# Feed-forward of a decoder layer: the up projection by Strassen's seven products on three equal token chunks, the down projection as a pass of its own

## The chip, the cores and the metric

The kernel runs on one core of a Trainium2 chip. The metric is device time in microseconds (us), from the first to the last instruction of one launch; less is better.

## The reference

One inference step of a decoder layer, for a prompt of 2048 tokens and for 8 sample tokens with a paged cache. Ahead of the feed-forward there are the input projection, three mixers (sparse attention with an indexer, pooling, attention to a memory) and the output projection with its residual. The change is in the last part:

```python
D_MODEL = 1024; D_FF = 2816; CONV_WIDTH = 3
def conv_ffn(up_ext, cw, cb, wd):
    T = up_ext.shape[1] - (CONV_WIDTH - 1)
    c = cb
    for j in range(CONV_WIDTH):
        c = c + cw[j] * up_ext[:, j:j + T]
    g, val = c[..., :D_FF], c[..., D_FF:]
    return (jax.nn.silu(g) * val) @ wd
...
up = rmsnorm(xp, norm2_g[l]) @ w_up[l]        # 2048 x 1024 by 1024 x 5632
up_ext = jnp.pad(up, ((0, 0), (CONV_WIDTH - 1, 0), (0, 0)))
xp = xp + conv_ffn(up_ext, conv_w[l], conv_b[l], w_down[l])
```

The sample tokens go through the same feed-forward, each with two past rows of its own for the convolution. Everything is float32.

## The kernel before

Each float32 operand of a product is split into a high and a low part, and a product is three matmuls: high by high, high by low, low by high. The splitting is a helper: ScalarE copies the high part (L224), VectorE subtracts it from the raw value (L225). The kernel is written in a framework that schedules: each engine works through a queue whose order is fixed when the program is built, by priorities that follow the order of the code; code under a raised number (`cur_priority += 1500`) gives way to as many instructions that come later.

After the output projection the second norm's result `h` (1024 channels, 8 groups of 128) is the right operand of the up projection. The feed-forward (L1600 and on) goes over three chunks of tokens, with bounds 0, 768, 1546 and 2048, the last with the 8 sample tokens. The first chunk's high and low parts (`fhh`, `fhl`) and its residual rows (`yacc`) stay on chip from the output projection on; those of later chunks are loaded from `h_d` and `x1_d` in memory. In a chunk the loop goes over 22 blocks `f` of 128 hidden units, and in a block:

- for the gate and the value (`j`): 512 KB of weights `wr` are loaded and split into `uh` and `ul` (128x1024), and the up projection (L1675 to L1677) adds 8 channel groups x 3 matmuls in PSUM (`upg`, `upv`), in two column pieces of 384 to 390, or one of 512 in the last chunk;
- the convolution takes its bias and last tap on ScalarE (L1679), the other taps on VectorE (L1680, L1682), each reading PSUM; then Silu on ScalarE (L1691), gate by value on GpSimd (L1692, `ct`), the high part `ah` on ScalarE and the low part `al` on VectorE;
- 512 KB of down weights `dr` are split into `dh` and `dl`. Every two blocks the down projection (L1717 to L1719, 512 columns) sums the two in PSUM (`py`), and VectorE adds that to `yacc` (L1720, 408 times). The rows of `yacc` are written out after the last block.

The sample tokens' mixers are traced ahead of this with 1500 instructions of lower priority, so they run beside the first two chunks: the indexer's scores over the cache (products `ipr` on GpSimd, L1244, summed by VectorE to `dots`, L1246), a search for the 256 best (L1285 and on), gathers, attention (`sw`, L1488 and L1506), the output projection (`swo`), the norm and the write of `h_d` for the third chunk (L1574).

## Time and profile before

| what | value |
|---|---|
| time, median of 3 runs | 2964.07 us (2961.45 to 2965.29) |
| the profiled execution, span | 2975.3 us, of mean granted clock 0.970 |
| TensorE, VectorE, GpSimd, ScalarE busy | 94%, 75%, 40%, 46% of the span |
| the feed-forward | 1373.8 us to the end |
| DMA over the whole span | 301.68 MB, 101 GB/s on average |

A busy time counts the instructions that the hardware profiler recorded; matmuls overlap one another, so their durations add up to more than the time they take, and the distance of successive starts is the price of one. "PE" is TensorE, "DVE" VectorE, "POOL" GpSimd, "ACT" ScalarE, "SP" the engine whose queue issues most transfers. The granted clock is a share of TensorE's full clock of 2.4 GHz, of which 1.2 GHz is the other level. An arrow in a row names what ended the idle time ahead of the instructions.

### The profile page before, as it was taken

To read this page: it belongs to the slowest core of one execution; us is meant where nothing else is said; L and a number is where in the kernel's file an instruction comes from. 1 tells how busy PE (TensorE), PEld (TensorE's weight loads), DVE (VectorE), ACT (ScalarE), POOL (GpSimd) and SP (SyncE) were. 2 spreads that over 40 slices of the span, in tenths; PEclk is the share of its full clock that TensorE was granted. 3 is DMA by queue.
4 is the path that set the end of the run, shared out by engine and by line. 5 is a ranking of instruction groups with operands and counts; after the bars stand their busy time and mean duration, and the time that the engine had idled before them with its cause. 6 is when DMAs were issued, how large, how long until landed. Compare 5 with 4: busy or idle time off the path is not lost.

```text
span 2975.3 us, 41646 instructions
## 1 busy us (share of the span) xinstructions
PE 2787.9 (94%) x14707; PEld 2428.2 (82%) x14707; DVE 2241.5 (75%) x4459; ACT 1365.5 (46%) x2307; POOL 1187.9 (40%) x1097
## 2 busy tenths in 40 slices
PE   8988788869999999999999999999989999999997
PEld 7877456658988988888988888989878889878886
DVE  5788987967888888446899989898787665666554
ACT  5667686457777777345222222232223333233332
POOL 2333434835745564002888998310436100000000
PEclk9999899879999999999999999999999999999999
DMA  5321334372213223653222222233343322243331
GB/s 183 124 91 54 124 101 123 102 215 80 82 55 99 62 83 99 190 149 115 71 74 75 86 64 73 69 122 121 96 129 92 109 80 82 82 153 106 93 92 53
DMA packets 310311, 301.68 MB, mean 101 GB/s; under 512 B 27444, under 2 KB 272245, under 8 KB 309317
## 3 DMA queue, kind: packets, MB, share of 16 engines
q1 hardware_dynamic: 305236, 285.28, 31.2%
q0 software_dynamic: 4864, 13.73, 1.6%
q8 instruction: 116, 1.90, 0.3%
q14 instruction: 95, 0.77, 0.1%
HBM read 236.36 MB, written 62.89 MB: 101 GB/s over the span
## 4 chain that ended last, share of the span: by engine, by line
PE 58%; DVE 12%; POOL 6%; DMA 3%; issue 2%; ACT 1%; SPq 0%; DVEq 0%; ACTq 0%; POOLq 0%
POOL ipr L1244 4%; PE py L1717 4%; PE upv L1677 4%; PE upv L1675 4%; PE py L1719 4%; PE upv L1676 4%; PE py L1718 4%; PE upg L1677 4%; PE upg L1675 4%; PE upg L1676 4%; PE apt L1055 3%; PE as L1038 2%; DVE dots L1246 2%; PE ax L1058 2%; PE ax L1059 2%
## 5 line engine op out<-in xcount | busy, mean ns | idle before, releaser
L1244 POOL TENSOR_TENSOR ipr<-G,qbc 128x512 f32<-128x512 f32 x256 | 371.1, 1479 | 66.4 <-DVE dots L1246 55.4
L1032 POOL TENSOR_TENSOR t<-R,first 128x128 f32<-128x128 f32 (+15 forms) x128 | 289.0, 2290 | 209.4 <-PE apt L1055 178.9
L1692 POOL TENSOR_TENSOR ct<-ct,ct 128x768 f32<-128x768 f32 (+2 forms) x65 | 118.6, 1824 | 623.8 <-DVE ct L1686 305.6
L1720 DVE TENSOR_TENSOR yacc<-yacc,py 128x512 f32<-128x512 f32 (+1 forms) x408 | 273.1, 680 | 117.8 <-PE py L1719 95.6
L1717 PE MATMUL py<-dh,ah 128*128 128x512 f32 (+1 forms) x704 | 279.8, 399 | 16.0 <-DVE yacc L1720 10.7
L1719 PE MATMUL py<-dh,al 128*128 128x512 f32 (+1 forms) x704 | 275.3, 397 | 3.9 <-DVE al L1697 3.9
L1718 PE MATMUL py<-dl,ah 128*128 128x512 f32 (+1 forms) x704 | 278.1, 395 | 0.0
L224 ACT ACTIVATE uh<-wr 128x1024 fp32r<-128x1024 f32 x132 | 139.6, 1058 | 292.9 <-PE upv L1676 97.3
L1676 PE MATMUL upg<-fhl,uh 128*128 128x390 f32 (+3 forms) x748 | 258.0, 345 | 5.0 <-issue 3.0
L225 DVE TENSOR_TENSOR ul<-wr,uh 128x1024 fp32r<-128x1024 f32 x132 | 176.7, 1339 | 110.4 <-ACT uh L224 110.2
L1676 PE MATMUL upv<-fhl,uh 128*128 128x390 f32 (+3 forms) x748 | 256.9, 343 | 0.0
L1675 PE MATMUL upg<-fhh,uh 128*128 128x390 f32 (+2 forms) x704 | 241.0, 342 | 5.2 <-DVE ct L1682 3.5
L1675 PE MATMUL upv<-fhh,uh 128*128 128x390 f32 (+2 forms) x704 | 240.1, 341 | 3.5 <-ACT ct L1679 2.0
L1677 PE MATMUL upg<-fhh,ul 128*128 128x390 f32 (+2 forms) x704 | 240.7, 342 | 2.8 <-issue 2.8
L1677 PE MATMUL upv<-fhh,ul 128*128 128x390 f32 (+2 forms) x704 | 239.4, 340 | 0.0
L225 DVE TENSOR_TENSOR pl<-apt,ph 128x512 fp32r<-128x512 f32 (+1 forms) x320 | 204.2, 658 | 24.2 <-ACT ph L224 21.9
L1040 DVE CUSTOM_DVE_ANT_0 t<-as,t 128x512 f32<-128x512 f32 (+11 forms) x320 | 189.8, 606 | 41.9 <-PE as L1039 36.7
L224 ACT ACTIVATE ph<-apt 128x512 fp32r<-128x512 f32 (+1 forms) x320 | 173.1, 581 | 62.0 <-PE apt L1055 32.5
L1246 DVE TENSOR_REDUCE dots<-ipr 128x16 f32<-128x512 f32 x256 | 171.8, 679 | 27.5 <-POOL ipr L1244 27.2
L1717 PEld LDWEIGHTS py<-dh,ah 128*128 128x128 f32 (+1 forms) x704 | 132.7, 189 | 44.5 <-DVE yacc L1720 16.5
L1055 PE MATMUL apt<-ident,t 128*128 128x128 f32 x1088 | 164.9, 274 | 3.4 <-DVE pl L225 1.9
L353 ACT ACTIVATE rl<-isc 128x768 f32<-128x768 f32 (+9 forms) x176 | 138.0, 822 | 59.7 <-PE isc L350 42.9
(578 smaller groups left out, 7676.1 us busy)
## 6 DMA issues: line engine op xcount, KB each, us to landing
wr<-in_w_up_dram SPq DMA_DIRECT2D x132, 512.0 KB
dr<-in_w_down_dram SPq DMA_DIRECT2D x66, 512.0 KB
xt<-in_x_prompt_dram SPq DMA_DIRECT2D x16, 512.0 KB
xh_d<-xh SPq DMA_DIRECT2D x16, 512.0 KB
xl_d<-xl SPq DMA_DIRECT2D x16, 512.0 KB
xh<-xh_d SPq DMA_DIRECT2D x16, 512.0 KB
xl<-xl_d SPq DMA_DIRECT2D x16, 512.0 KB
qa<-qh_d SPq DMA_DIRECT2D x64, 128.0 KB
```

The source lines that it names most:

```text
L224: nc.scalar.activation(hi, ps, AF.Copy)
L225: nc.vector.tensor_tensor(lo, ps, hi.bitcast(F32), op=OP.subtract)
L1032: nc.gpsimd.tensor_tensor(t[:, :N], backward(R[j][:, :N]), nsel[b], op=OP.add)
L1055: nc.tensor.transpose(pt[:, c, j * 128:j * 128 + 128], pn[j][:, (k + c) * 128:(k + c) * 128 + 128], ident)
L1244: nc.gpsimd.tensor_tensor(pr, G[:, u * 512:u * 512 + 512].rearrange("p (k d) -> p k d", d=32), qbc[:, c, None, 32 * h:32 * h + 32].to_broa ...
L1675: nc.tensor.matmul(d, uh[:, k], hh(k, a, e), start=(k == 0), stop=False)
L1676: nc.tensor.matmul(d, uh[:, k], hl(k, a, e), start=False, stop=False)
L1677: nc.tensor.matmul(d, ul[:, k], hh(k, a, e), start=False, stop=(k == KC - 1))
L1717: nc.tensor.matmul(py[:p], ah[:, r0:r0 + p], dh[:, cs], start=(i == 0), stop=False)
L1718: nc.tensor.matmul(py[:p], ah[:, r0:r0 + p], dl[:, cs], start=False, stop=False)
L1719: nc.tensor.matmul(py[:p], al[:, r0:r0 + p], dh[:, cs], start=False, stop=e)
L1720: nc.vector.tensor_tensor(y[:w, cs], y[:w, cs], py[:w], op=OP.add)
```

## The change

The tokens are cut into three equal chunks: 688, 688 and 680 (the last with the sample tokens). A chunk's right operand is a matrix of two channel halves by two token halves; the left one has two channel halves by gate and value of a block. Their product is made by Strassen's scheme in Winograd's form: seven products of half size instead of eight, each of 4 channel groups x 3 matmuls at 344 (340) columns. The seven right operands (`b11`, `t1`, `t2`, `b21`, `t3`, `b22`, `t4`) are made once a chunk (`operands`: eight subtractions on GpSimd, and 14 splits) and stay on chip. The seven left operands are made for every block: three are parts of the weights as loaded, four are sums `s` made on GpSimd. Partial products are summed in place in PSUM and put together into `u` in SBUF by four copies on ScalarE and three additions on VectorE. The convolution reads `u`. The activation is written to memory (`act_d`).

The down projection is a pass of its own for each chunk and each half of the output columns: it loads the activation and the down weights, splits them, and sums all 22 blocks in PSUM; at the end the residual is loaded, added by VectorE and written. All 16 blocks of the output projection now write `x1_d` and `h_d`. The sample tokens' mixers get 5500 in place of 1500. Comments are removed throughout.

```diff
-    bounds = [0, 768, 1546, 2048]
+    chunks = [(0, 344), (688, 344), (1376, 340)]
...
+    def operands(ci, stage):
+        for kk in range(0, 4, 2):
+            get(raw("b11"), 0, 0)
+            get(x, 0, 1)
+            get(raw("b22"), 1, 1)
+            get(raw("b21"), 1, 0)
+            G(y, x, raw("b11"), op=OP.subtract)
+            split_psum(raw("b11"), h("b11"), l("b11"))
+            split_psum(y, h("t1"), l("t1"))
+            G(x, raw("b22"), x, op=OP.subtract)
+            G(y, raw("b22"), y, op=OP.subtract)
+            split_psum(y, h("t2"), l("t2"))
+            G(y, raw("b21"), y, op=OP.subtract)
+            split_psum(raw("b21"), h("b21"), l("b21"))
+            split_psum(x, h("t3"), l("t3"))
+            split_psum(raw("b22"), h("b22"), l("b22"))
+            split_psum(y, h("t4"), l("t4"))
...
-    tc.cur_priority += 1500
+    tc.cur_priority += 5500
...
+                product(pa, two_parts(g0), "b11", True)
+                nc.scalar.activation(x1, pa[:, :N], AF.Copy)
+                G(s, v0, v1, op=OP.add)
+                product(pc, two_parts(s), "t1", True)
+                nc.scalar.activation(x5, pc[:, :N], AF.Copy)
+                G(s, s, g0, op=OP.subtract)
+                product(pa, two_parts(s), "t2", False)
+                nc.scalar.activation(u2, pa[:, :N], AF.Copy)
+                product(pb, two_parts(g1_), "b21", True)
+                nc.vector.tensor_tensor(u[:, 0, lo], pb[:, :N], x1, op=OP.add)
+                G(s3, g0, v0, op=OP.subtract)
+                product(pa, two_parts(s3), "t3", False)
+                nc.vector.tensor_tensor(u[:, 1, hi], pa[:, :N], x5, op=OP.add)
+                G(s, g1_, s, op=OP.subtract)
+                product(pc, two_parts(s), "b22", False)
+                nc.vector.tensor_tensor(u[:, 0, hi], pc[:, :N], u2, op=OP.add)
+                product(pa, two_parts(v1), "t4", False)
+                nc.scalar.activation(u[:, 1, lo], pa[:, :N], AF.Copy)
...
-                    nc.vector.scalar_tensor_tensor(c_[:, :n], pu[:, o + 1:o + 1 + n], cw(1, fc), c_[:, :n],
+                    nc.vector.scalar_tensor_tensor(c_[:, :n], u[:, j, 1:1 + n], cw(1, fc), c_[:, :n],
...
+                dma(act_d[f, :, t0:t0 + m], ct[0][:, :m])
...
-                            nc.vector.tensor_tensor(y[:w, cs], y[:w, cs], py[:w], op=OP.add)
...
+        def down(t0, nb, rest, c, spare=None, fr=None):
+            for f in range(NF):
+                dr = fd.tile([128, 512], F32, name="dr", bufs=3)
+                dma(dr, I["w_down"][0, f * 128:f * 128 + 128, cs])
...
+                split_psum(dr, dh, dl)
...
+                dma(raw, act_d[f, :, t0:t0 + k + rest])
...
+                for i in range(nb):
+                    b = slice(i * 128, i * 128 + 128)
+                    nc.tensor.matmul(ys[i], ah[:, b], dh, start=s, stop=False)
+                    nc.tensor.matmul(ys[i], ah[:, b], dl, start=False, stop=False)
+                    nc.tensor.matmul(ys[i], al[:, b], dh, start=False, stop=e)
...
+                nc.vector.tensor_tensor(x, ys[i], x, op=OP.add)
+                dma(y_p[0, r:r + 128, cs], x)
...
+        for ci in range(2):
+            up(ci)
+            down(640 * ci, 5, 0, 0)
+            operands(ci + 1, stage)
+            down(640 * ci, 5, 0, 1)
+        up(2)
...
+        for c in range(2):
+            down(1280, 6, NS, c, fpx, fr)
```

A down pass takes 640 tokens of the first two chunks each, and the third the last 776. Some places of the fixed order follow. On GpSimd, in the first blocks of the first chunk, before (`G` are gathers of cache rows):

```order
L1244 TENSOR_TENSOR ipr<-G,qbc 128x512 x10
L1238 DMA G<-in_cache_idx_k_dram,gidx 128x1024
L1692 TENSOR_TENSOR ct_19851<-ct_19851,ct_19904 128x768
L1244 TENSOR_TENSOR ipr<-G,qbc 128x512 x17
L1238 DMA G<-in_cache_idx_k_dram,gidx 128x1024
L1692 TENSOR_TENSOR ct_19981<-ct_19981,ct_20034 128x768
```

There only one product `ct` a block stands between the `ipr`.

On GpSimd in the first chunk's up pass, now (`s` are the sums of weights, `hal` keeps the last two columns for the next chunk):

```order
L1671 TENSOR_TENSOR s<-s,wr 128x512
L1250 TENSOR_TENSOR ipr<-G,qbc 128x512 x2
L1244 DMA G<-in_cache_idx_k_dram,gidx 128x1024
L1701 TENSOR_TENSOR ct<-ct 128x688
L1663 MEMSET u 128x2x2
L1679 TENSOR_TENSOR s<-wr,s 128x512
L1250 TENSOR_TENSOR ipr<-G,qbc 128x512 x2
L1668 TENSOR_TENSOR s<-wr 128x512
L1676 TENSOR_TENSOR s<-wr 128x512
L1250 TENSOR_TENSOR ipr<-G,qbc 128x512 x2
```

Between two `ipr` there now stand one or two sums on whose splits TensorE's products rest; of the 256, 149 come before the last `ct` of this pass and 97 in the first down pass.

On SP's queue at the end of the second chunk's down pass, now (`out_dram<-ct` are the output rows, `swo` the sample tokens' output weights, `sh` their norm, `u` and `b22l` the third chunk's operands, `act_d<-ct` its first activation):

```order
L1755 DMA out_dram<-ct 128x512 x2
L1509 DMA Vg<-in_cache_mem_v_dram 128x2x256 x8
L1526 DMA B_18498<-s_B_d 8x296
L1529 DMA sr<-in_state_pool_dram 120x256
L1560 DMA swo<-in_w_out_dram 128x512 x2
L1566 DMA sxt<-in_x_sample_dram 8x1024
L1560 DMA swo<-in_w_out_dram 128x512 x14
L1573 DMA x_d<-sxt 8x1024
L1582 DMA h_d<-sh 128x8x8
```

The loads for the sample tokens' last steps now stand behind the output rows of that pass; before, they stood between loads of feed-forward weights.

On TensorE behind that pass's last matmul, now (`srow` are past rows of the convolution):

```order
L1563 MATMUL sb<-swh,smx_18534 40x512
L1564 MATMUL sb<-swl,smx_18534 40x512
L1123 MATMUL sa<-ident,shn 128x8 x8
L1595 MATMUL sa<-ident,srow 128x128 x4
L1653 MATMUL py<-t1h,wh 128x340
L1654 MATMUL py<-b11l,wh 128x340
L1655 MATMUL py<-b11h,wl 128x340
```

Before, the same transposes stood amid the second chunk's products:

```order
L1677 MATMUL upg<-fhh,ul 128x390
L1095 MATMUL sa<-ident,shn 128x8 x4
L1675 MATMUL upg<-fhh,uh 128x390
L1676 MATMUL upg<-fhl,uh 128x390
L1677 MATMUL upg<-fhh,ul 128x390
```

What moved is that the sample tokens' last steps are no longer between matmuls of the feed-forward; the third chunk's up pass stands behind them on both queues.

## Rows read from the trace of the kernel before

**Rows 1.** The page, busy time and share of the span of each engine.

```profile
PE 2787.9 (94%) x14707; PEld 2428.2 (82%) x14707; DVE 2241.5 (75%) x4459; ACT 1365.5 (46%) x2307; POOL 1187.9 (40%) x1097
```

**Rows 2.** Busy time by stretch, a column for each engine, then granted clock and DMA.

```profile
600.00:700.00 100.00, 72.08 (x384) 59.28 (x383) 65.36 (x184) 57.11 (x135) 44.17 (x50) 0.78 0.64 183
...
1290.00:1390.00 100.00, 100.00 (x499) 86.23 (x497) 49.69 (x172) 50.27 (x97) 3.34 (x3) 1.00 0.41 123
...
1390.00:1500.00 110.00, 105.36 (x555) 98.75 (x555) 96.45 (x120) 32.08 (x37) 90.76 (x62) 1.00 0.29 86
...
1600.00:1700.00 100.00, 96.11 (x496) 88.53 (x496) 90.74 (x113) 25.85 (x30) 89.63 (x62) 1.00 0.24 75
...
2400.00:2900.00 500.00, 499.92 (x2300) 420.95 (x2299) 301.96 (x431) 167.35 (x265) 38.96 (x32) 1.00 0.32 98
```

**Rows 3.** TensorE's timeline (start, duration, line, operation), at 256, 384 and 512 columns.

```profile
880.11 0.28 PE L1058 MATMUL ax<-ph,vst 128*128 128x256 f32 x1
...
880.58 0.28 PE L1058 MATMUL ax<-ph,vst 128*128 128x256 f32 x1
...
1453.06 0.34 PE L1675 MATMUL upv<-fhh,uh 128*128 128x384 f32 x1
...
1453.95 0.33 PE L1677 MATMUL upv<-fhh,ul 128*128 128x384 f32 x1
...
2700.89 0.39 PE L1675 MATMUL upg<-fxh,uh 128*128 128x512 f32 x1
...
2705.93 0.39 PE L1676 MATMUL upg<-fhl,uh 128*128 128x512 f32 x1
```

**Rows 4.** GpSimd's costliest group, 1390 to 1900 us.

```profile
L1244 POOL TENSOR_TENSOR ipr<-G,qbc 128x512 f32<-128x512 f32 x256 | 371.1, 1479 | 66.4 <-DVE dots L1246 55.4 <-DMA qbc<-s_iq_d 9.7 <-DVE sn L1227 0.7
```

**Rows 5.** GpSimd's timeline, three places, and VectorE's beside the first.

```profile
1411.14 7.28 POOL L1244 TENSOR_TENSOR ipr<-G,qbc 128x512 f32<-128x512 f32 x5 [0.69 <-DVE sn L1227]
...
1418.38 1.84 POOL L1692 TENSOR_TENSOR ct<-ct,ct 128x768 f32<-128x768 f32 x1
...
1438.02 2.56 POOL L1244 TENSOR_TENSOR ipr<-G,qbc 128x512 f32<-128x512 f32 x2 [0.39 <-DVE dots L1246]
...
1413.08 1.69 DVE L225 TENSOR_TENSOR ul<-wr,uh 128x1024 fp32r<-128x1024 f32 x1
```

**Rows 6.** VectorE's groups, 1390 to 1900 us, beside a busy GpSimd.

```profile
L1246 DVE TENSOR_REDUCE dots<-ipr 128x16 f32<-128x512 f32 x256 | 171.8, 679 | 27.5 <-POOL ipr L1244 27.2
...
L225 DVE TENSOR_TENSOR ul<-wr,uh 128x1024 fp32r<-128x1024 f32 x40 | 63.8, 1595 | 1.8 <-ACT uh L224 1.8
...
L1680 DVE SCALAR_TENSOR_TENSOR ct<-upv,convc,ct 128x768 f32<-128x768 f32 x20 | 20.1, 1005 | 0.0
```

**Rows 7.** The same, 2430 to 2900 us, beside an idle GpSimd.

```profile
L225 DVE TENSOR_TENSOR ul<-wr,uh 128x1024 fp32r<-128x1024 f32 x49 | 60.0, 1224 | 80.4 <-ACT uh L224 80.4
```

**Rows 8.** The sample tokens' search on VectorE, 1880 to 2080 us.

```profile
L1285 DVE TENSOR_TENSOR sge<-sS,scand 128x1548 f32<-128x1548 f32 x15 | 26.5, 1769 | 0.3
L1287 DVE TENSOR_REDUCE scn<-sge 128x12 f32<-128x1548 f32 x15 | 26.4, 1759 | 0.0
```

**Rows 9.** The sample tokens' last steps: GpSimd's timeline, then that of SP's queue.

```profile
2294.74 1.18 POOL L1506 TENSOR_TENSOR sw<-Vg,PM 128x256 f32<-128x256 f32 x2
...
2330.47 0.26 POOL L1546 MEMSET smx<- 128x192 f32 x1
...
2439.86 0.37 SPq L1574 DMA_DIRECT2D h_d<-sh  x1
```

**Rows 10.** The border: TensorE's timeline; writer of `h_d` (first, last start); chain of waits.

```profile
1373.79 0.34 PE L1675 MATMUL upg<-fhh,uh 128*128 128x386 f32 x1
...
L1176 SPq DMA_DIRECT2D h_d<-hn x1: 370/370/370, 1388.4 to 1388.4; - x1
...
1469.99 3.67 DMA dr<-in_w_down_dram
```

**Rows 11.** The end on VectorE, its timeline.

```profile
2956.50 4.87 DVE L1720 TENSOR_TENSOR yacc<-yacc,py 128x512 f32<-128x512 f32 x8 [1.72 <-PE py L1719]
```

More of the change, by code (lines that the diff above doesn't have):

```diff
@@ L1127, in tile_decoder @@
             split_psum(raw, woh[k], wol[k])
-        n0 = bounds[1] // TQ
-        for i, b in enumerate(list(range(n0, NB - 1)) + list(range(n0)) + [NB - 1]):
+        order = [4, 5, 2, 3, 0, 1, 6, 7, 14, 15, 12, 13, 10, 11, 8, 9]
+        for i, b in enumerate(order):
             q0 = b * TQ
@@ L1136, in tile_decoder @@
             split_psum(mt, mh, ml)
-            xt = load(b)
+            xt = load(i)
             dma(xt, xp[q0:q0 + TQ])
@@ L1178, in tile_decoder @@
-        hb = ow.tile([128, KC, 2], F32, name="hb", bufs=1)
-        for kk in range(4):
-            hi, lo = (t[kk][:, :, bounds[1]:bounds[1] + 2].bitcast(F32) for t in (fhh, fhl))
-            nc.vector.tensor_tensor(hb[:, 2 * kk:2 * kk + 2], hi, lo, op=OP.add)
-        dma(h_d[:, :, bounds[1] - 2:bounds[1]].rearrange("k p t -> p k t"), hb)
-    f0 = pool("f0", stack=ffst)
-    for nm in ("wr", "uh", "ul"):
-        f0.tile([128, KC, 128], F32 if nm == "wr" else F32R, name=nm)
+            dma(x1_d[q0:q0 + TQ], x1)
@@ new lines, in tile_decoder, with put @@
+            h = ox.tile([128, KC, 128], F32, name="h", bufs=2)
+            def put(half, ph):
+                for i in range(4):
+                    k = half * 4 + i
+                    if half:
+                        nc.scalar.activation(h[:, k], ph[:, i], AF.Copy, scale=g2(k))
+                    else:
+                        nc.vector.tensor_scalar(h[:, k], ph[:, i], g2(k), None, op0=OP.mult)
+            second_norm(x1, TQ, hn, ops, put)
+            dma(h_d[:, :, q0:q0 + TQ].rearrange("k p t -> p k t"), h)
@@ L1541, in tile_decoder @@
         dma(pool_s[0, :, 14, :], s_B_d[:, 40:296])
+        s4.close()
+        s4 = ExitStack()
+        sp2 = pool("spo", bufs=2, side="right", stack=s4)
         po = [sps.tile([128, 512], F32, name=nm) for nm in ("sa", "sb")]
```

308 lines of the change are left out of this document (138 added, 170 removed).

## The prediction

> **What bounds the kernel now.** I read the page first: TensorE is busy for 94% of the span, VectorE for 75%, GpSimd for 40% [rows 1]. These are averages, so the table by stretch comes next. The feed-forward begins at 1373.8 us [rows 10] and runs to the end. In 1390 to 1900 three engines are near full at once: TensorE 96%, VectorE 88 to 91%, GpSimd 83 to 90%; from 2400 on TensorE alone is, with VectorE at 60% and GpSimd at 8% [rows 2]. So TensorE sets the time now, but in the first third of the feed-forward there is no room on the other two: the sample tokens' scores (256 products `ipr` on GpSimd, 256 sums `dots` on VectorE) lie there. The reader is to see in [rows 4] that `ipr` is 371.1 us of GpSimd's time, and in [rows 6] that `dots` is 171.8 us of VectorE's.
>
> **What the change takes from TensorE.** Starts of successive matmuls give the price: at 256 columns four steps take 0.47 us (0.1175 each), at 384 five take 0.89 (0.178), at 512 twenty-two take 5.04 (0.229) [rows 3]. By the line between the first two, 344 columns cost 0.159 and 340 cost 0.157; every one of these has its own weight load, so no load sets a floor above 0.1175. The up projection before is 2112 matmuls of 384 or 386 columns, 2112 of 390 and 1056 of 512 (those of 390 taken at the price of 384): 4224 x 0.178 + 1056 x 0.229 = 994 us. After, it is 84 a block of weights: 3696 x 0.159 + 1848 x 0.157 = 878, in three passes of 294, 294 and 290 (13.4 us a block). The arithmetic saves **116 us**. The down projection keeps its 2200 matmuls of 512 columns: 2200 x 0.229 = 504 us, as 151 after each of the first two chunks (660 each) and 202 after the third (880). The 408 additions into `yacc` go from VectorE; they become 32 at the ends of the passes.
>
> **What it adds.** Seven operands a block, four of them made on GpSimd (`s`, 128x512, two SBUF inputs): 264 in all. No row has this operation, but `ipr` has the same size and inputs: two alone take 2.56 us, 1.28 each [rows 5]. The two taps of the convolution on VectorE (`ct`) now have both inputs in SBUF, where one was in PSUM. Seven splits of 512 columns take the place of two of 1024 a block, 1.75 times the elements. The activation goes to memory and comes back twice; the loads are counted at nothing, since the DMA engines are 24 to 32% busy in the feed-forward [rows 2] and a load of 3.67 us [rows 10] has a ring of three buffers over blocks of 6.9 us (151 / 22). If that cover went, a block would take its load and two splits of at most 0.8 one after another, 3.67 + 1.6 = 5.3, still under 6.9.
>
> **Pass by pass**, from TensorE's last matmul of the output projection at 1373.8:
>
> (1) *Border.* The first `wr` tiles lie over tiles of the output projection, and on SP's queue they stand behind the last block's `h_d`. That write starts at 1388.4 now [rows 10]; with a load of 512 KB (3.67, [rows 10]) and a split, the first product can start near 1394. **20 us** where there was nothing; no less than 12 if the norm comes earlier, 22 at most, and no gain, because TensorE waits for nothing there now.
>
> (2) *First up pass.* In GpSimd's fixed order 149 of the 256 `ipr` stand between the 88 sums `s`, six or eight to a block. Bare: 149 x 1.28 + 88 x 1.28 + 22 products `ct` of 688 columns (1.84 x 688/768 = 1.65, [rows 5]) + about 14 for gathers and copies = **354 us**, against 294 of TensorE. TensorE waits for `s` by way of the splits, so GpSimd is the bound in any case. To this comes what the two vector engines take from each other: five `ipr` beside one `ul` took 7.28 us instead of 6.4, and that `ul` took 1.69 instead of 1.22 [rows 5, 7]; over the whole stretch `ul` is 1595 ns against 1224 [rows 6, 7], while a tap (`ct`) with one input in PSUM stays at 1005 [rows 6]. So 0.88 of 1.22, some 0.7 of the VectorE time with two SBUF inputs, is passed on to GpSimd. After, that time is 154 splits `wl` x 0.61 (half of 1.224) + 88 taps x 0.90 (1005 x 688/768) = 173 us. Between nothing and all of it, 354 to 527; with 0.7 it is **475**. VectorE by itself, stretched by 1595/1224 = 1.3, has 154 x 0.80 + 88 x 1.17 + 149 sums `dots` x 0.68 [rows 6] and 66 additions `u` x 0.41 (344/512 of 4.87 / 8, [rows 11]): 354, less than that. TensorE is then 62% busy; a stretch with 72% had the granted clock at 0.78 [rows 2], but 294 / 0.78 = 377 would still hide under 475.
>
> The Trainium skill ("SBUF — State Buffer", section "SBUF: two separate sides") says that an operation of VectorE with two SBUF inputs and one of GpSimd that reads SBUF exclude each other for a whole instruction. The rows above agree in kind and stop at 0.7; by the rule the pass would take 527.
>
> (3) *First down pass.* GpSimd has 97 more `ipr` and eight subtractions for the next operands: 124 + 13; VectorE's two-input time is some 70 (43 `dl` of 512, 41 `al` of 640, 14 splits of 688), 0.7 of it is 49: **188** against TensorE's 151. Between 152 and 207.
>
> (4) *Second up pass.* GpSimd is down to 169 + 0.7 x 173 = 290, just under TensorE's 294. VectorE carries 7 x 0.61 + 4 x 0.90 + 3 x 0.41 = 9.1 a block, and in 16 blocks one step of the search, 3.5 us in its two large operations alone [rows 8], with short ones and waits for TensorE's sums near 5: with a little stretch about 15 us a block there against 13.4. **330**; 300 to 350.
>
> (5) *Second down pass.* 151 of TensorE, VectorE half full: **155**.
>
> (6) *Wait for the sample tokens.* The third chunk holds them, so its operands need their `h_d`. Their mixers now give way to 5,500 instructions, and in the order the tail stands behind the whole second down pass on TensorE; on SP's queue the memory values and all 16 pieces of the output weights stand behind this pass's output writes. Now the tail runs under feed-forward work: memory values from 2294.7 to 2330.5, and from there 109 us to `h_d` at 2439.9 [rows 9], none of it TensorE's wait. After, nothing covers it (the third pass's products, its `wr` loads and its first sums are queued behind it on TensorE, SP and GpSimd): 36 + 109 as now, less what runs quicker alone, plus some 16 us of subtractions and splits for the operands. **140**; 80 if half is quicker, 190 if part of the gathers is late too.
>
> (7) *Third up pass* 290 on TensorE, with GpSimd and VectorE close behind: **305**. (8) *Third down pass* **205**. (9) *End:* eight additions take 4.87 us now [rows 11], and 14 us lie between the last matmul and the end; after, six additions and their writes: **14**.
>
> The sum: 20 + 475 + 188 + 330 + 155 + 140 + 305 + 205 + 14 = 1832, and with 1373.8 it is 3206 us of profiled span. The profiled execution before, 2975.3, lies 11.2 above the median of 2964.07; less that, **3195 us**.
>
> **Rivals.** *A. The saving outlives the waits (faster).* One mechanism: the locking on the SBUF side costs nothing because VectorE's operations fall into GpSimd's gaps (GpSimd has 66.4 us idle before `ipr` now, [rows 4]), and the tail is half as long alone. Then the passes are 354, 152, 300, 153, 293, 203, with 12 at the border, a tail of 80 and 13 at the end: 2934, that is 2923. It decides where the losses in (1), (2) and (6) together stay under about 150. For it: the GpSimd idle; against it: the 1.69 us of [rows 5]. With no loss at all the time would be 2964 - 116 = 2848, but the 354 alone forbids that.
>
> *B. The exclusion is whole (slower still).* 527 in (2), 207 in (3), 345 in (4), 329 in (7): 110 more, 3305. The exclusion of the Trainium skill's page "SBUF — State Buffer", section "SBUF: two separate sides", is this rival's rule. For it: in 1390 to 1500 GpSimd and VectorE are full at once and both stretched; against it: the 0.88 of 1.22.
>
> *C. Shorter matmuls don't pay (the change doesn't do what it says).* If 344 columns went at 0.178, the second and third passes would be 35 us longer each: 3265. [rows 3] speaks against it.
>
> **How the numbers follow.** My case, with its terms between their ends: 0.63, some 3050 to 3270. B: 0.18, 3270 to 3390. C: 0.03. A: 0.12, 2880 to 2955. About the same as before: 0.04. A measurement tells some 0.2% of this kernel apart, 6 us. Faster 0.12, same 0.04, slower 0.84. The range that leaves out about 2 in 10 goes into A below and B above: 2930 to 3330.
>
> **What would show it.** Right: in the first 470 us of the feed-forward TensorE near 62% busy, waiting for splits of `s`, GpSimd near 95%, `wl` well over 0.61; after the second down pass a stretch of over 80 us with almost no matmul; the second and third taps slower beside a busy GpSimd than the 0.90 of their size. Wrong: an up pass under 350 us while `ipr` is running, or the third pass's first products less than 50 us behind the second down pass. The 0.159 is checked by successive starts.

## The result, and the profile after

The changed kernel takes **3351.41 us** (median of 4 runs, 3349.27 to 3352.45) against 2962.76 us of the kernel before (median of 4 runs, 2957.47 to 2965.29): the ratio is 1.131, with an interval of 1.1294 to 1.1327. The forecast was 3195 us, with a range of 2930 to 3330. The direction held, and the loss is 389 us where about 230 were forecast. The time lies above the range. It lies 46 us above the sum of rival B (3305), and within the interval that the prediction gave B (3270 to 3390).

The profiled execution has a span of 3350.7 us. The page's first row (busy time, share of the span and instructions of each engine) answers to [rows 1]:

```profile
PE 2824.1 (84%) x14971; PEld 2430.6 (73%) x14971; DVE 2652.0 (79%) x4781; ACT 1653.3 (49%) x2963; POOL 1787.9 (53%) x1575
```

TensorE is busy about as long as before (2824 us against 2788). VectorE has 410 us more, GpSimd 600 us more. An operation that stands still for another engine counts as busy too. So the time went into TensorE's waits, and the question is for which engine it waited. The table by stretch, cut at the passes' ends on TensorE (columns: stretch, length, then busy time of TensorE's matmuls and weight loads, VectorE, ScalarE and GpSimd with their instructions, then granted clock, DMA share, GB/s), answers to [rows 2]:

```profile
1376.00:1406.00 30.00, 4.03 (x18) 3.19 (x17) 10.22 (x38) 9.06 (x20) 6.82 (x8) 0.58 0.71 196
1406.00:1883.00 477.00, 368.07 (x1864) 342.77 (x1865) 449.48 (x473) 183.91 (x322) 432.20 (x303) 0.85 0.27 81
1883.00:2105.00 222.00, 173.39 (x673) 130.07 (x672) 212.74 (x219) 70.52 (x115) 173.73 (x113) 0.93 0.47 151
2105.00:2481.00 376.00, 324.27 (x1884) 305.00 (x1882) 366.96 (x487) 174.97 (x308) 238.06 (x172) 0.96 0.30 92
2481.00:2663.00 182.00, 159.75 (x664) 125.17 (x664) 133.17 (x308) 61.98 (x100) 79.62 (x72) 0.95 0.71 215
2663.00:2800.00 137.00, 58.07 (x163) 26.96 (x162) 62.65 (x117) 32.60 (x55) 50.08 (x59) 0.56 0.28 85
2800.00:3119.00 319.00, 289.50 (x1772) 279.90 (x1772) 277.32 (x342) 166.76 (x294) 212.51 (x187) 0.98 0.29 92
3119.00:3335.00 216.00, 209.99 (x889) 160.74 (x887) 80.23 (x141) 61.63 (x91) 7.26 (x45) 0.98 0.45 142
```

The lines are, in order: border, first up, first down, second up, second down, the wait for the sample tokens, third up, third down. The reader is to see the column of VectorE: 94%, 96% and 98% busy in the first up, first down and second up pass. GpSimd, which the prediction held for the bound, is at 91%, 78% and 63% there. The list of waits (who waits for whom, total us, times, longest) has three lines of TensorE over the whole feed-forward, and one of ScalarE in the first up pass:

```profile
PE py L1655 <- DVE wl L225: 84.3, 61, 4.9
PE py L1653 <- ACT wh L224: 67.5, 32, 15.2
PE py L1740 <- DVE dl L225: 53.1, 34, 6.3
...
ACT wh L224 <- POOL s L1668: 76.0, 21, 5.3
```

The first and third are waits for VectorE. The second is not: ScalarE makes `wh`, and the last line shows it waiting in turn for GpSimd's first sum of a block. In the first up pass TensorE waits 65.7 us for `wl` and 56.1 us for `wh`, so both engines hold it there. From the first down pass on VectorE is clearly the fuller (96% against 78%).

VectorE's costliest groups (line, engine, operation, tile, shapes, count; then busy us, mean ns of one; then its idle time before) answer to [rows 6, 7]. First the first up pass, here up to 1862 us, some 20 us before its last products (expectations below that speak of passes of 456, 243 and 358 us count by this cut):

```profile
L225 DVE TENSOR_TENSOR wl<-s,wh 128x512 fp32r<-128x512 f32 x85 | 112.8, 1327 | 2.9 <-ACT wh L224 2.9
...
L225 DVE TENSOR_TENSOR wl<-wr,wh 128x512 fp32r<-128x512 f32 x64 | 89.8, 1405 | 0.0
L1690 DVE SCALAR_TENSOR_TENSOR ct<-u,convc,ct 128x688 f32<-128x688 f32 x41 | 62.1, 1515 | 4.4 <-ACT ct L1689 4.0
L1692 DVE SCALAR_TENSOR_TENSOR ct<-u,convc,ct 128x688 f32<-128x688 f32 x40 | 56.7, 1417 | 0.2
```

Then the first down pass (1862 to 2104.6), and one row of the second up pass (2104.6 to 2463):

```profile
L1732 DVE TENSOR_TENSOR al<-al,ah 128x640 fp32r<-128x640 f32 x42 | 62.9, 1498 | 2.0 <-ACT ah L1728 2.0
L225 DVE TENSOR_TENSOR dl<-dr,dh 128x512 fp32r<-128x512 f32 x43 | 60.7, 1413 | 0.8 <-ACT dh L224 0.8
...
L225 DVE TENSOR_TENSOR wl<-s,wh 128x512 fp32r<-128x512 f32 x79 | 73.4, 929 | 6.2 <-ACT wh L224 6.2
```

A split of 512 columns takes 1.33 to 1.41 us in the first up and first down pass and 0.93 in the second up pass. The prediction had 0.80 for the first and 0.61 for the last.

### The profile page after: what moved, and what is told of

It reads as the page before. It is cut to its first block, busy times and chain, and to the rows that moved or that the text cites. A ratio compares the mean times of both kernels' runs of the same rounds, so it can differ in the third digit from the quotient of the medians.

```text
span 3350.7 us, 45058 instructions
## 1 busy us (share of the span) xinstructions
PE 2824.1 (84%) x14971; PEld 2430.6 (73%) x14971; DVE 2652.0 (79%) x4781; ACT 1653.3 (49%) x2963; POOL 1787.9 (53%) x1575
## 5 line engine op out<-in xcount | busy, mean ns | idle before, releaser
L1740 PE MATMUL py<-dl,ah 128*128 128x512 f32 x704 | 284.4, 413 | 53.4 <-DVE dl L225 53.1
L225 DVE TENSOR_TENSOR wl<-s,wh 128x512 fp32r<-128x512 f32 x264 | 278.0, 1053 | 33.4 <-ACT wh L224 33.4
L224 ACT ACTIVATE wh<-s 128x512 fp32r<-128x512 f32 x264 | 164.8, 626 | 271.7 <-POOL s L1668 138.9
L1741 PE MATMUL py<-dh,al 128*128 128x512 f32 x704 | 274.8, 406 | 2.1 <-DVE al L1732 2.1
L225 DVE TENSOR_TENSOR wl<-wr,wh 128x512 fp32r<-128x512 f32 x198 | 222.5, 1131 | 0.0
L1739 PE MATMUL py<-dh,ah 128*128 128x512 f32 x704 | 204.0, 404 | 17.0 <-ACT ah L1728 7.7
L1740 PEld LDWEIGHTS py<-dl,ah 128*128 128x128 f32 x704 | 137.7, 196 | 102.5 <-DVE dl L225 70.8
L1690 DVE SCALAR_TENSOR_TENSOR ct<-u,convc,ct 128x688 f32<-128x688 f32 (+1 forms) x132 | 180.7, 1369 | 27.7 <-ACT ct L1689 26.9
L1739 PEld LDWEIGHTS py<-dh,ah 128*128 128x128 f32 x704 | 135.0, 193 | 55.8 <-ACT ah L1728 9.9
L1692 DVE SCALAR_TENSOR_TENSOR ct<-u,convc,ct 128x688 f32<-128x688 f32 (+1 forms) x132 | 165.8, 1256 | 0.5
L1044 ACT ACTIVATE t<-t,amn 128x128 f32<-128x128 f32 (+15 forms) x128 | 154.4, 1208 | 20.6 <-DVE amn L1043 13.1
```

The lines of the kernel that those rows point to most:

```text
L224: nc.scalar.activation(hi, ps, AF.Copy)
L225: nc.vector.tensor_tensor(lo, ps, hi.bitcast(F32), op=OP.subtract)
L1690: nc.vector.scalar_tensor_tensor(c_[:, :n], u[:, j, 1:1 + n], cw(1, fc), c_[:, :n], op0=OP.mult, op1=OP.add)
L1692: nc.vector.scalar_tensor_tensor(c_[:, :n], u[:, j, 0:n], cw(0, fc), c_[:, :n], op0=OP.mult, op1=OP.add)
L1739: nc.tensor.matmul(ys[i], ah[:, b], dh, start=s, stop=False)
L1740: nc.tensor.matmul(ys[i], ah[:, b], dl, start=False, stop=False)
```

## Experiments

The theory behind the forecast was that GpSimd and VectorE, with operands in SBUF, hold each other up, and that the sample tokens' chain stands alone. The rivals, after the result: the change of passes alone costs the time, or the order does.

**What the two engines take from each other.** A kernel of its own, with nothing of the decoder: 24 sums on GpSimd of the size of `s`, alone and beside one kind of VectorE operation at a time.

```diff
+    def two():
+        last["v"] = out()
+        V.tensor_tensor(last["v"], raw, hi, op=OP.subtract)
...
+    def psum():
+        last["v"] = out()
+        V.tensor_tensor(last["v"], bank, hi, op=OP.subtract)
...
+    def tap():
+        V.scalar_tensor_tensor(ct, u[:, 1:689], 0.5, ct, op0=OP.mult, op1=OP.add)
...
+    def pool():
+        last["g"] = p.tile([128, 512], F32, name="gs", bufs=2)
+        G.tensor_tensor(last["g"], ga, gb, op=OP.add)
```

`two` is a split with both inputs in SBUF, `psum` the same with one input in PSUM, `tap` a tap of 688 columns, `pool` a sum of weights.

> The disputed cost by itself, without the decoder (the kernel computes none of it): eleven stretches, one after another. First VectorE alone: 24 subtractions 128x512 with two SBUF inputs, 24 with one input in PSUM, 24 with one SBUF input, 24 sums along rows, 16 taps 128x688; then GpSimd alone, 24 additions 128x512; then each of VectorE's five beside those 24. Whole exclusion: the stretch with the subtractions takes 24 x 0.6 + 24 x 1.28 = some 45 us, a subtraction is near 1.9 us beside an addition, an addition near 1.9; with one input in PSUM or one SBUF input or the sums 31 us and unstretched; the taps some 16 x 0.9 + 31 = 45. With 0.7 as in the prediction: some 41 and a smaller stretch on VectorE's side, 0.8 for a subtraction. None: 31.

It ran once. Groups of six stretches: the splits alone, the sums alone, both together, the sums beside splits with an input in PSUM, the taps alone, the taps beside the sums:

```profile
L123 DVE TENSOR_TENSOR lo<-raw,hi 128x512 fp32r<-128x512 f32 x24 | 14.7, 686 | 0.0
...
L143 POOL TENSOR_TENSOR gs<-ga,gb 128x512 f32<-128x512 f32 x24 | 29.3, 1260 | 0.1
...
L143 POOL TENSOR_TENSOR gs<-ga,gb 128x512 f32<-128x512 f32 x24 | 40.0, 1702 | 0.1
L123 DVE TENSOR_TENSOR lo<-raw,hi 128x512 fp32r<-128x512 f32 x24 | 39.0, 1699 | 0.0
...
L143 POOL TENSOR_TENSOR gs<-ga,gb 128x512 f32<-128x512 f32 x24 | 29.6, 1268 | 0.1
L127 DVE TENSOR_TENSOR lo<-bank,hi 128x512 fp32r<-128x512 f32 x24 | 14.4, 677 | 0.0
...
L138 DVE SCALAR_TENSOR_TENSOR ct<-u,ct 128x688 f32<-128x688 f32 x16 | 14.0, 875 | 0.6
...
L138 DVE SCALAR_TENSOR_TENSOR ct<-u,ct 128x688 f32<-128x688 f32 x16 | 28.4, 1778 | 0.5
```

GpSimd's 24 sums go from 29.3 to 40.0 us: 10.7 of VectorE's 14.7, 73%, are passed on. That is the 0.7 that the prediction read from [rows 5, 6, 7]. For VectorE the price is quite another, and not the 0.8 us expected: the splits go from 686 to 1699 ns, level with the sums beside them (1702 ns), as when the two take turns. The taps go from 875 to 1778 ns. So an operation of 512 columns loses 1.01 us and one of 688 columns 0.90: in this mix the wait does not grow with the size. An input in PSUM costs neither engine anything (677 and 1268 ns).

The Trainium skill ("SBUF — State Buffer", section "SBUF: two separate sides") has the two exclude each other for a whole instruction; that would be, as an estimate, 14.7 + 29.3 = 44.0 us here, and 40.0 were measured.

The kernel before had a row that shows the same, VectorE's scaling of the scores in 1390 to 1900 us:

```profile
L1248 DVE TENSOR_TENSOR dots<-dots,wB 128x256 f32<-128x256 f32 x16 | 35.9, 2241 | 0.5 <-ACT dots L1247 0.5
```

It has only 256 columns and two SBUF inputs, and takes 2241 ns beside `ipr`; in the next run, without `ipr`, it takes 697. The prediction took its factor from splits of 1024 columns alone, which lost 0.37 us.

**The products off GpSimd.** The sample tokens' 256 `ipr` left out; VectorE sums the gathered rows themselves.

```diff
-                        pr = sp2.tile([128, 16, 32], F32, name="ipr")
-                        nc.gpsimd.tensor_tensor(pr, G[:, u * 512:u * 512 + 512].rearrange("p (k d) -> p k d", d=32),
-                                                qbc[:, c, None, 32 * h:32 * h + 32].to_broadcast([128, 16, 32]), op=OP.mult)
+                        pr = G[:, u * 512:u * 512 + 512].rearrange("p (k d) -> p k d", d=32)
```

> The changed kernel without the 256 products `ipr` on GpSimd; VectorE's sums `dots` read the gathered rows themselves, so the sample tokens' scores are another set, of the same size. Theory 1 (VectorE's operations with two SBUF inputs and GpSimd's reads of SBUF keep each other out): `wl` falls from 1.33 to 1.40 us in the first up pass to about 0.9, as it is in the second pass where GpSimd has the sums alone; the first up pass from 456 us to 310 to 330, the first down pass from 243 to 160 to 175, the whole by 200 to 230, to 3120 to 3150. Theory 2 (VectorE simply has more to do, and its operations are long for a reason of their own): `wl` stays at 1.3, both passes change by less than 30 us.

Measured: 3189.41 us, 1.0756 (1.0723 to 1.079) of before. The first up pass by stretch, and two groups of VectorE in it:

```profile
1405.00:1869.00 464.00, 355.71 (x1890) 329.70 (x1890) 458.40 (x694) 185.78 (x332) 220.05 (x170) 0.89 0.30 90
...
L1250 DVE TENSOR_REDUCE dots<-G 128x16 f32<-128x512 f32 x245 | 150.8, 672 | 0.0
L225 DVE TENSOR_TENSOR wl<-s,wh 128x512 fp32r<-128x512 f32 x89 | 69.4, 780 | 3.0 <-ACT wh L224 3.0
```

GpSimd falls from 432 to 220 us, the split from 1327 to 780 ns: the splits did wait for GpSimd. Yet the pass is only 13 us shorter. Without `ipr` to wait for, 245 of the 256 `dots` (143 before) and the start of the search move into it, and VectorE is 99% busy. The expected pass length (310 to 330) was missed, and the miss told more than a hit: with GpSimd half idle, VectorE alone still holds this pass at its length. The gain of 162 us came later, chiefly from the tail: the sample tokens' chain began earlier, and the wait of 137 us ahead of the third up pass is gone.

**Splits that don't wait.** In the up passes `wl` is made by an operation with one SBUF input of the same size.

```diff
-                    split_psum(w, *p)
+                    nc.scalar.activation(p[0], w, AF.Copy)
+                    nc.vector.tensor_scalar(p[1], w, 2.0 ** -13, 0.0, op0=OP.mult, op1=OP.add,
+                                            accum_out=acc1[:, 0:1])
```

`wl` now needs no `wh` either, so a wait for ScalarE goes with it; VectorE idled 2.9 us for that in the first up pass.

> The changed kernel with the 462 low parts `wl` of the weights made by an operation with one SBUF input (the weight times a constant), so the product's low parts are other numbers; count, size, engines and all of GpSimd's work stay. Theory 1: `wl` near 0.65 us in every pass, `ipr` down from 1.64 to about 1.45, the first up pass 456 to about 400, the second 358 to about 330, the first down pass as it is (243), the whole 80 to 100 less, 3250 to 3270. Theory 2: `wl` as long as before and no pass changes by more than 15 us.

Measured: 3233.33 us, 1.0904 (1.0873 to 1.0936), a little beyond what was expected. The first and the third up pass by stretch, and a group of the first:

```profile
1403.00:1824.00 421.00, 345.33 (x1867) 329.25 (x1868) 367.55 (x628) 182.84 (x321) 379.52 (x304) 0.87 0.30 92
2705.00:2996.00 291.00, 284.45 (x1792) 280.60 (x1791) 237.72 (x490) 170.36 (x301) 175.94 (x190) 0.99 0.32 99
...
L1646 DVE TENSOR_SCALAR_CACHE_REDUCE wl<-wr 128x512 fp32r<-128x512 f32 x67 | 45.4, 678 | 0.8
```

The split is at 678 ns, `ipr` at 1457 in place of 1643. The first up pass is 56 us shorter, the second 45, the third 28; in the third, at 291 us, TensorE is now busy for 284. Relieving the splits alone gives back 118 us of the 389. That is net of what moves elsewhere: the first tap, still with two SBUF inputs, goes from 1515 to 1730 ns in the first up pass.

**No sums on GpSimd.** The four sums a block left out; the same seven products and splits from the weights as loaded.

```diff
-                G(s, v0, v1, op=OP.add)
-                product(pc, two_parts(s), "t1", True)
+                product(pc, two_parts(v0), "t1", True)
...
-                G(s, s, g0, op=OP.subtract)
-                product(pa, two_parts(s), "t2", False)
+                product(pa, two_parts(v1), "t2", False)
...
```

> The changed kernel without the 264 sums `s` on GpSimd; parts of the weights as loaded take their place, so the seven products are of other matrices. GpSimd loses 88 operations of some 1.5 us in the first up pass and the chain from sum to split to product is gone. If the keeping out sets the pass: 456 to about 390, since `ipr` still meets `wl` and the taps; the second 358 to about 325, the third 312 to about 295; the whole 3250 or so. If TensorE's wait for the sums' chain sets it: the first pass near 310. If neither, under 20 us in all.

Measured: 3201.79 us, 1.0798 (1.0762 to 1.0834), some 50 us more gain than expected. First and third up pass:

```profile
1409.00:1806.00 397.00, 336.82 (x1872) 322.98 (x1872) 396.40 (x461) 186.92 (x330) 269.42 (x197) 0.91 0.33 100
2685.00:2973.00 288.00, 284.43 (x1811) 283.64 (x1812) 234.06 (x352) 172.90 (x303) 86.33 (x112) 0.99 0.33 100
```

GpSimd has 163 us less in the first pass, and VectorE still fills it whole. The sums on GpSimd cost 150 us, though VectorE is the fuller engine. In the first pass a split falls to 1152 ns, so part of this is VectorE's waiting; how much is the shorter chain from sum to split to product, the run doesn't tell.

**The passes with eight products.** The seven products undone, the three chunks, the separate down passes and the 5500 kept.

```diff
-                product(pa, two_parts(g0), "b11", True)
...
-                product(pa, two_parts(v1), "t4", False)
+                wg0, wg1, wv0, wv1 = (two_parts(w) for w in (g0, g1_, v0, v1))
+                for d, w0, w1, o0, o1 in ((pa, wg0, wg1, "b11", "b21"), (pc, wg0, wg1, "t1", "b22"),
+                                          (pb, wv0, wv1, "b11", "b21"), (pd, wv0, wv1, "t1", "b22")):
+                    product(d, w0, o0, True)
+                    product(d, w1, o1, False)
...
```

> The changed kernel with the seven products undone and the rest kept: the same three chunks and passes, eight products a block (96 matmuls of 344 columns in place of 84), no sums on GpSimd, four splits in place of seven, no subtractions for the operands. TensorE's arithmetic alone: 42 us longer a pass, 126 in all, 3475. VectorE and its stretch as the bound: the first up pass falls from 477 us to about 370, the second from 376 to about 350, the third's products from 312 to about 340, the down passes keep their length; the whole some 3240 to 3270.

Measured: 3135.39 us, 1.0575 (1.0545 to 1.0604), over 100 us under what was expected. The first up pass came out longer than expected (418 us, not 370), the second and third shorter (335 and 318, not 350 and 340), and the wait, which the expectation leaves out, fell to 47 us. First up, second up, the wait, third up:

```profile
1389.00:1807.00 418.00, 358.84 (x2111) 353.02 (x2112) 395.60 (x450) 128.41 (x215) 377.22 (x273) 0.93 0.31 95
...
2016.00:2351.00 335.00, 331.00 (x2097) 330.67 (x2097) 239.84 (x438) 127.23 (x195) 99.90 (x108) 0.99 0.39 115
...
2543.00:2590.00 47.00, 22.06 (x67) 10.81 (x66) 17.55 (x42) 13.32 (x21) 0.00 (x0) 0.58 0.43 130
2590.00:2908.00 318.00, 318.00 (x2038) 317.64 (x2037) 170.30 (x267) 128.10 (x190) 70.89 (x107) 1.00 0.28 89
```

This divides the loss. The passes with eight products cost 3135.4 − 2965.4 = **170 us** against before (the kernel before, run beside it, took 2965.4); Strassen's scheme, put on top, 3351.4 − 3135.4 = **216 us** more. By stretches of the two profiled executions, 59 of it lie in the first up pass, 41 in the second, and 90 in the wait, 137 us in place of 47. Some 18 of these go to the third chunk's operands, as the next run shows. The rest is the largest part: not a pass that grew, but the sample tokens' chain coming later.

In the second and third up pass TensorE works almost without a gap at a clock of 0.99 and 1.00. The third takes 318 us with its larger count of matmuls, the seven products take 319: what the scheme saves there on TensorE it loses in waits, even where no `ipr` is left. They are other waits than in the first pass: in the third TensorE stands 19 us for ScalarE's copies (`fx`, `fu`, `u`) and 10 us for VectorE's additions `u`, which empty its banks of PSUM.

**The scheme in the last chunk alone**, where GpSimd and VectorE have most room.

```diff
+            if ci < 2:
...
+                if ci < 2:
+                    wg0, wg1, wv0, wv1 = (two_parts(w) for w in (g0, g1_, v0, v1))
...
+                else:
+                    product(pa, two_parts(g0), "b11", True)
...
```

The first two chunks keep the eight products, the third has the seven.

> The kernel with plain products (3135), and the seven products in the third up pass alone, where neither the scores nor the search lie on VectorE and GpSimd. If the scheme pays where these two are free: the third pass's products go from about 337 us to about 312, less some 12 of subtractions for the operands that nothing covers: 3115 to 3130. If it doesn't: 3135 to 3160.

Measured: 3167.46 us, 1.0684 (1.0619 to 1.0749), 32 us more than with eight products throughout, and 7 above the range expected for a scheme that doesn't pay. Its third up pass:

```profile
2605.00:2929.00 324.00, 292.66 (x1785) 283.16 (x1784) 280.28 (x344) 169.47 (x297) 216.03 (x189) 0.98 0.29 89
```

It takes 324 against 318 us, and the wait ahead of it, 65 us, is 18 longer; the third chunk's operands take eight subtractions and 14 splits there, in place of eight splits. With all but the last of the sample tokens' work done, the scheme doesn't pay either.

**The third chunk without the sample tokens.** Its operands are read from eight tokens further ahead, so that they don't need the sample tokens' `h_d`; the rows computed for the sample tokens are then not theirs.

```diff
-            get = lambda dst, kh, half: dma(dst, h_d[4 * kh + kk:4 * kh + kk + 2, :, t0 + half * n:t0 + half * n + n]
+            b0 = t0 - 8 * (ci == 2)
+            get = lambda dst, kh, half: dma(dst, h_d[4 * kh + kk:4 * kh + kk + 2, :, b0 + half * n:b0 + half * n + n]
```

> The changed kernel with the third chunk's operands read eight tokens earlier, so they need nothing of the sample tokens (the last rows' results are others). Theory 1 on the 140 us between the second down pass and the third up pass (they are the wait for the sample tokens' `h_d`): this stretch falls to under 25 us, the third up pass takes 10 to 40 more because the sample tokens' last steps now lie beside it, the whole 3230 to 3260. Rival (the stretch is the queue of SP behind the output rows, or work on VectorE and GpSimd that has to be done in any case): no more than 30 us less.

Measured: 3338.11 us, 1.1258 (1.1209 to 1.1306): 13 us less, so the expected 90 to 120 fell, and the rival was right. Two stretches behind the second down pass:

```profile
2668.00:2710.00 42.00, 36.71 (x217) 34.19 (x215) 35.10 (x41) 17.45 (x33) 34.77 (x39) 0.96 0.45 138
2710.00:2820.00 110.00, 49.07 (x157) 24.51 (x156) 50.51 (x107) 27.69 (x48) 28.37 (x39) 0.57 0.24 76
```

The third up pass begins at once, and 42 us later comes a stretch of 110 us in which TensorE is busy for 49. The data dependence alone was not what held it: the sample tokens' matmuls are in order in TensorE's queue, and what they wait for comes no sooner (`h_d` is written at 2800 us, 36 later than in the changed kernel). In the changed kernel, the timeline of SP's queue (start, duration, line, operation, count) shows that chain, from the memory values to the third chunk's weights:

```profile
2685.50 22.21 SPq L1509 DMA_DIRECT2D Vg<-in_cache_mem_v_dram  x8
...
2724.06 26.76 SPq L1560 DMA_DIRECT2D swo<-in_w_out_dram  x14
...
2764.45 0.38 SPq L1582 DMA_DIRECT2D h_d<-sh  x1
...
2799.02 4.09 SPq L1638 DMA_DIRECT2D wr<-in_w_up_dram  x2
```

**Both up passes ahead of both down passes**, so that the down passes and the tail have the same work beside them in another order.

```diff
-        for ci in range(2):
-            up(ci)
-            down(640 * ci, 5, 0, 0)
-            operands(ci + 1, stage)
-            down(640 * ci, 5, 0, 1)
+        up(0)
+        operands(1, stage)
+        up(1)
+        down(0, 5, 0, 0)
+        operands(2, stage)
+        down(0, 5, 0, 1)
+        down(640, 5, 0, 0)
+        down(640, 5, 0, 1)
```

> The changed kernel with the two first up passes ahead of the two first down passes, nothing else changed. If the 140 us ahead of the third up pass are a chain of the sample tokens' steps that has too little other work beside it: the stretch falls to 50 to 80 us, the 97 products `ipr` of the first down pass go into the second up pass (376 to about 430), and the first down pass falls from 222 to about 165; the whole 3230 to 3290, with 20 us of wait between the two up passes. If VectorE's whole load sets the time up to the third pass: within 25 us of 3351.

Measured: 3381.54 us, 1.14 (1.1377 to 1.1423). The two up passes, the two down passes, the wait:

```profile
1405.00:2383.00 978.00, 733.13 (x3732) 680.36 (x3733) 915.43 (x986) 378.42 (x657) 840.42 (x587) 0.84 0.25 79
2383.00:2738.00 355.00, 322.93 (x1374) 250.65 (x1372) 259.45 (x523) 121.79 (x197) 108.49 (x110) 0.98 0.66 206
2738.00:2845.00 107.00, 54.93 (x188) 32.32 (x187) 58.66 (x108) 32.70 (x53) 26.63 (x25) 0.62 0.29 93
```

The gain didn't come; it was 30 us slower, 5 more than the second theory allowed. VectorE's work up to the wait is the same, 915 + 259 = 1175 us against 1162 in the changed kernel (the four passes of the table above), and the two up passes have it at 94%. That speaks for the theory that VectorE's load sets it: moving passes doesn't make the load smaller. Up to the wait this order takes 1333 us against 1257, with VectorE at only 73% in the two down passes; the wait is 30 us shorter.

**The number 1500 in place of 5500**, in the changed kernel.

```diff
-    tc.cur_priority += 5500
+    tc.cur_priority += 1500
```

> The changed kernel with the sample tokens' mixers at 1500 as before. In the order they move by less than a hundred matmuls. If the order's structure holds them: within 20 us of 3351. If the number cost here what it costs in the kernel before (73 us): 3270 to 3300.

Measured: 3338.69 us, 1.1261 (1.1207 to 1.1316), 13 us less. With the seven products the number isn't where the 389 us are.

**The number 5500 in the kernel before.**

```diff
-    tc.cur_priority += 1500
+    tc.cur_priority += 5500
```

> The kernel before with the sample tokens' mixers at 5500 in place of 1500, one part of the change alone. If the number is what puts the tail ahead of the third chunk: 40 to 120 us more than before. If the order comes from the structure of the passes: within 20 us of before.

Measured: 3037.95 us, 1.0246 (1.0218 to 1.0274): 73 us more. The stretch where TensorE waits for the sample tokens:

```profile
2600.00:2700.00 100.00, 61.96 (x233) 42.82 (x234) 42.28 (x76) 28.09 (x44) 3.88 (x3) 0.74 0.26 78
```

In the kernel before, with the down projection in the same loop, a later sample chain does cost. In the changed kernel the tail is late with either number. With eight products in passes, 1500 was not run, so some of the 170 us, by an estimate from these 73 up to as much, may belong to the number; that isn't shown.

**No reloads.** The down passes read one fixed tile in place of the activation, whose loads are left out.

```diff
-                raw = al[:, :k + rest].bitcast(F32)
-                dma(raw, act_d[f, :, t0:t0 + k + rest])
+                raw = act1[:, :k + rest]
```

> The changed kernel with the down passes' activation taken from one tile that is loaded once, so the 132 loads from `act_d` and the wait for the last activation of an up pass are gone (the outputs are of other values; the splits, the matmuls and the writes to `act_d` stay). If the trip through memory costs what the second and third down passes have over TensorE's 151 and 202 us: these fall from 182 and 216 (each with some 12 us between the passes) to about 160 and 206, the first, where VectorE is full, from 222 to 210 at the least, the whole 40 to 70 less, 3280 to 3310. If the second is long because of the sample tokens' work on VectorE: within 20 us of 3351.

Measured: 3556.24 us, 1.1995 (1.1935 to 1.2056): 205 us slower with less to do. The stretch between the first up and down pass, and a down pass:

```profile
1876.00:2340.00 464.00, 32.14 (x96) 16.23 (x96) 291.94 (x547) 29.89 (x53) 272.52 (x254) 0.50 0.16 44
...
2829.00:2998.00 169.00, 160.97 (x703) 130.44 (x702) 102.83 (x123) 70.00 (x111) 29.29 (x18) 0.99 0.34 109
```

The edit changed the order, so it doesn't answer its question: the rest of the sample tokens' chain now stands in one piece ahead of the first down pass, 464 us in which TensorE is busy for 32. What it does show is the size of that chain when nothing covers it, and a down pass of 169 us without it. The second up pass, freed of the whole chain, took 319 us, as long as the third pass of the changed kernel: that is the seven products' own length here, against 290 of TensorE's arithmetic (1848 matmuls at 0.157).

## Why the prediction was right in direction and too small

**Pass by pass.** Each measured length against its term: border 30 (20), first up 477 (475), first down 222 (188), second up 376 (330), second down 182 (155), wait 137 (140), third up 319 (305), third down 216 (205), end 16 (14), and the feed-forward began 2 us later. The differences, 2 + 10 + 2 + 34 + 46 + 27 − 3 + 14 + 11 + 2, are 145 us: span 3350.7 against the 3206 of the sum. The other 11 us up to the median are the deduction for the profiled execution; this time it agrees with the median. Two terms don't follow from their own parts: in (3) 124 + 13 + 49 is 186, not 188, and in (4) 16 blocks at 15 us and 6 at 13.4 are 320, not 330. Neither changes the picture.

**The step that failed** is in (2): "VectorE by itself, stretched by 1595/1224 = 1.3 … 354, less than that". VectorE was busy for 449 us. The factor 1.3 came from splits of 1024 columns with a wait of 0.37 us in 1.60. But the wait is for each operation, not for each element: the mixing kernel shows 1.0 us for a split of 512 columns and 0.9 for a tap of 688 beside a GpSimd that never rests, and in the first up pass it is 1.36 − 0.68, some 0.7, for a split. Halving the split left its wait no smaller, and the change makes seven of them a block in place of two, and gives the taps two SBUF inputs. Measured, a split took 1.36 where 0.80 was put, a tap 1.47 where 1.17 was, an addition `u` 0.50 where 0.41 was.

**Why (2) still came out at 477.** In the prediction the larger of two sums counts, and GpSimd's was 475, of which 432 were measured; VectorE's, put at 354, happened to lie as high, at 449. That is luck: if GpSimd alone had been the bound, the kernel without `ipr` would have brought this pass far down, and it took 13 us off it.

**Where VectorE was left out or put too low, the length was wrong.** In (3) only GpSimd was summed; VectorE was 96% busy with splits at 1.41 and 1.50 us, and TensorE's wait for `dl` there is 43.2 us of the 222. In (4) "with a little stretch about 15 us a block" in 16 blocks is the term that was too small: splits of 0.93 and taps of 1.35 in every block keep VectorE at 98%. These two are 80 of the 145 us. In (7) TensorE is idle for 29.5 of 319 us, where 15 were put.

**(5)** was costed as TensorE's 151 alone. It took 182 us, of which TensorE waits for 22: 10.0 for `dl`, 6.8 for the activation's high part, 3.5 for a step of the search that stands in its queue. In the working on the DMA there is a slip: a block of a down pass was put at 6.9 us, but a pass goes over the blocks once for each half of the columns, so it is 3.4. What that cost isn't shown, since the run without reloads changed the order; the third down pass, 216 us with TensorE busy for 210, leaves little for it.

**(1)** was 10 us short. **(6)** was right to 3 us in length and in where it lies, but not in its terms. GpSimd's timeline of the changed kernel answers to [rows 9], the first product of the memory values and the end of the last:

```profile
2692.43 1.18 POOL L1512 TENSOR_TENSOR sw<-Vg,PM 128x256 f32<-128x256 f32 x2 [2.31 <-issue]
...
2714.35 0.26 POOL L1555 MEMSET smx<- 128x192 f32 x1 [1.55 <-DVE svl L225]
```

The first 29 us, from 2663, go to gathered cache values that the sum of (6) put at nothing (only its upper end, 190, has gathers that are late). Then come 22 us of memory values (36 put), 50 to `h_d` (109 put, less what runs quicker alone), and 36 from there to the end of the wait (16 put). That these add up to 137 is luck. The order in the queues is borne out: with the data dependence gone, 42 us of the third pass come ahead, and the stretch stays.

**TensorE's price held.** Its timeline in the first up pass (start, duration, line, operation), two pairs of matmuls, 10 and 9 starts apart, answers to [rows 3]:

```profile
1476.90 0.32 PE L1653 MATMUL py<-t4h,wh 128*128 128x344 f32 x1
...
1478.47 0.32 PE L1653 MATMUL py<-t1h,wh 128*128 128x344 f32 x1
...
1473.64 0.49 PE L1653 MATMUL py<-b11h,wh 128*128 128x344 f32 x1
...
1476.22 0.49 PE L1653 MATMUL py<-t4h,wh 128*128 128x344 f32 x1
```

1.57 / 10 = 0.157 us at the full clock, where 0.159 was put: rival C fell. The second pair, 2.58 / 9 = 0.287, is at the lower level of 1.2 GHz (granted clock 0.50 from 1473.64 to 1476.22 us, 1.00 from 1476.90 to 1479.20). The mean of the pass is 0.85, where the prediction put 0.78; it doesn't seem to set the length, with TensorE waiting 122 us for `wl` and `wh`.

**The rivals.** A fell: no up pass of the changed kernel came near 300. By its time B was hit (3270 to 3390), but not by its passes: it has 527, 207, 345 and 329 us in (2), (3), (4) and (7), and 477, 222, 376 and 319 were measured. It named the right cause, and put its price on the wrong engine: whole exclusion adds to GpSimd, by the prediction 110 us; the mixing kernel shows 0.73 in place of 1 there, and the larger loss is VectorE's.

**What the change costs, by the runs.** Against 2965.4 us of the kernel before, run beside the kernel with eight products, the whole is 386 us: 170 belong to the passes and 216 to the seven products, 90 of these to the longer wait for the sample tokens. Leaving out the sums on GpSimd gives back 150, and splits that don't wait give back 118 (the two overlap and don't add). No version of the changed kernel that was run beats the kernel before.

Still open is how the 170 us divide between border, tail, reloads, the number 5500 and the larger load on VectorE. The run with eight products has a first up pass of 418 us, where 2112 matmuls at 0.157 would take 332. VectorE is 95% busy in it, and TensorE's longest wait there is 58.6 us for a copy by VectorE. Its first two down passes take 209 and 192 us, where 151 of TensorE's each were put. None of the runs takes the causes apart.

## To carry to other kernels

Where VectorE and GpSimd work side by side, count VectorE's operations with two SBUF inputs, and not only their elements: here each lost 0.5 to 1.0 us beside GpSimd's operations of 1.2 to 1.6 us, whether it had 512 or 688 columns, so making more and smaller ones has its price by number. Look for the shortest such operation in the trace before, not the longest. Sum every engine of a stretch at its stretched duration before naming the bound, and where two sums lie close, carry both into the neighbouring stretches. Ask what a fuller engine delays: here, from eight products to seven, the chain that came late cost more than any pass that grew. A scheme that saves an eighth of TensorE's products and pays in sums and splits on the other engines needs those engines to have room at that price; here they lacked it even in the chunk with the least other work.

## What the runs showed of the hardware

The exclusion isn't symmetric in its effect. Beside one another, 24 operations of each engine kept VectorE busy for 39.0 us and GpSimd for 40.0, so VectorE's took 2.7 times as long as alone and GpSimd's 1.4 times: in this mix the engine with the shorter operation falls to the pace of the other. With one input in PSUM, 24 operations took 14.4 us on VectorE, alone and beside GpSimd, and GpSimd's 29.6 against 29.3.

At the lower of TensorE's two clock levels, a matmul of 344 columns took 0.287 us against 0.157, 1.8 times, not twice. In stretches in which TensorE mostly waited, the granted clock's mean was 0.50 to 0.62 (the waits above); in those in which it worked through, 0.98 to 1.00.
